# Other cuts for the last row of a streamed Poisson loss: x 3136, 768, 192 and t 1600, 1536, 576, 384 columns

## Chip, cores, metric

The kernel runs on one core of one Trainium2 chip. The metric is the device time of one execution, in microseconds (us). All executions that are compared here ran at a granted clock of 1.00; those of several rounds are classed as fast, and the four single runs at the end of the experiments have the state "unknown", which a single run of a one-core program always has. Kernels are compared only within the same rounds.

## The reference

```
batch, dim = 1024, 4096            # both inputs float32
loss = np.exp(log_input) - target * log_input
return np.mean(loss, axis=-1)      # 1024 numbers
```

Partition p holds rows 8p to 8p+7. Below, "row" means one of these eight, so a row is 128 partitions by 4096 columns, and x is `log_input`, t is `target`.

## The kernel before

SyncE issues all loads on one queue: rows 0 to 3 of x, then of t, rows 4 and 5, row 6, and the last row in seven pieces whose sizes TAIL sets (in units of d/32 = 128 columns). ScalarE takes the exponential of each x piece and sums it, VectorE multiplies each t piece with x and sums it. The sums of the last row's pieces stand behind t's last columns as six extra columns, against an x of -1.0 there, so that VectorE's closing instruction multiplies the last t piece and adds up all partial sums in one go.

```
TAIL = [("x", 24), ("t", 12), ("t", 12), ("x", 6), ("t", 5), ("x", 2), ("t", 3)]
# ... (cut)
    for what, w in TAIL:
        loads.append((what, at[what], w * d // 32))
        at[what] += w * d // 32
# ... (cut: buffers, semaphores, the loads, the loop over x)
    for j, (lo, w, i) in enumerate(t_work):
        row = lo // d
        x_load = next(ix for a, wx, ix in x_work if a + wx >= lo + w)
        if j == 0 or x_load > t_work[j - 1][2]:
            nc.vector.wait_ge(landed[x_load], 16)
        if j < n_t - 1:
            nc.vector.tensor_tensor_reduce(...).wait_op(landed[i], 16, "sem-ge")...
        else:
            nc.vector.wait_ge(ones_done, 1)
            nc.vector.wait_ge(exp_done, n_x - 1)
            nc.vector.wait_ge(prod_done, n_t - 2)
            nc.vector.tensor_tensor_reduce(
                out=place("t", lo, w + n_parts), ...
                accum_out=all_loss[:, last_row : last_row + 1],
            ).wait_op(last_ready, 18, "sem-ge").then_inc(loss_done, 1)
```

`last_ready` reaches 18 when the last load (16), the last exponential (1) and the last product before the closing one (1) are done. A product waits for its own t piece and for the x piece that covers its last column.

## Time and profile before

| | before |
|---|---|
| time, median of 6 runs | 84.05 us (84.01 to 84.12) |
| span of the profiled execution | 82.9 us |
| share of 16 DMA engines in use | 95.5% |
| VectorE, ScalarE busy | 43%, 40% |

From the page of the kernel before, the DMA queue (packets, MB, share of 16 engines' span) and the chain that ended last (shares of the span by engine, then by line):

```profile
q1 hardware_dynamic: 2016, 33.56, 95.5%
...
DMA 72%; DVE 18%; issue 4%; SPq 3%; ACT 1%
DMA t_big<-in_target_dram 49%; DMA x_big<-in_log_input_dram 23%; DVE t_big L175 17%; SPq L129 3%; DVE t_big L193 1%; ACT e_dump L155 1%; DVE parts L175 0%; SPq L127 0%; DVE all_loss L193 0%
```

The chain is transfers, with compute (18% VectorE) only where a load has to wait for a buffer to come free while other transfers still run. ACT's 1% at its end is the one piece of compute that stands between the last transfer of the chain (the load of x3) and the closing instruction.

### The profile page before, as it was taken

The page shows a single profiled execution, that of the slowest core. Times are in us where ns is not written, and L with a number is a line of the kernel's source. Part 1 is how long each engine was busy: PE and PEld are TensorE (multiplying, and loading weights), DVE is VectorE, ACT ScalarE, POOL GpSimd, SP SyncE. Part 2 cuts the span into 40 slices and gives each one's busy share as a digit, 9 for nine tenths or more (in the row PEclk, how much of TensorE's full clock was granted, in tenths as well). Part 3 has the DMA queues.
Part 4 walks back from the last instruction along what each step waited for, and adds up shares of the span by engine and source line. Part 5 has one row for each costly group of instructions (what it writes and reads, how often), then busy time and mean ns, then how long its engine had stood idle before and what let it go on. Part 6 is the DMA issues. An engine that isn't in the chain of part 4 may idle for free.

```text
span 82.9 us, 131 instructions
## 1 busy us (share of the span) xinstructions
DVE 35.6 (43%) x22; ACT 33.2 (40%) x35; POOL 0.3 (0%) x5
## 2 busy tenths in 40 slices
DVE  0000000000000000000099999999469996994992
ACT  0500000000399920000000897979793496019460
POOL 0000000000000000000000000000000000000000
DMA  9199999929999992999699799899899999999950
GB/s 506 63 443 506 506 506 506 443 127 443 506 506 506 506 443 127 443 506 506 269 490 474 316 474 490 380 411 490 364 403 435 443 435 393 433 397 421 393 184 2
DMA packets 2016, 33.56 MB, mean 405 GB/s; under 512 B 352, under 2 KB 608, under 8 KB 1120
## 3 DMA queue, kind: packets, MB, share of 16 engines
q1 hardware_dynamic: 2016, 33.56, 95.5%
HBM read 33.55 MB, written 0.00 MB: 405 GB/s over the span
## 4 chain that ended last, share of the span: by engine, by line
DMA 72%; DVE 18%; issue 4%; SPq 3%; ACT 1%
DMA t_big<-in_target_dram 49%; DMA x_big<-in_log_input_dram 23%; DVE t_big L175 17%; SPq L129 3%; DVE t_big L193 1%; ACT e_dump L155 1%; DVE parts L175 0%; SPq L127 0%; DVE all_loss L193 0%
## 5 line engine op out<-in xcount | busy, mean ns | idle before, releaser
L175 DVE CUSTOM_DVE_ANT_0 t_big<-t_big,x_big 128x4096 f32<-128x4096 f32 (+2 forms) x8 | 26.2, 3306 | 43.8 <-DMA t_big<-in_target_dram 43.6
L155 ACT ACTIVATE e_dump<-x_big 128x4096 f32<-128x4096 f32 (+3 forms) x8 | 21.8, 2730 | 24.2 <-DMA x_big<-in_log_input_dram 24.0
L175 DVE CUSTOM_DVE_ANT_0 t_mid<-t_mid,x_mid 128x4096 f32<-128x4096 f32 x2 | 8.8, 4424 | 2.0 <-DMA t_mid<-in_target_dram 2.0
L141 ACT ACTIVATE join_dump<-parts 128x2 f32<-128x2 f32 x7 | 1.4, 203 | 20.4 <-DVE parts L175 20.4
L155 ACT ACTIVATE e_dump<-x_mid 128x4096 f32<-128x4096 f32 x2 | 7.1, 3568 | 0.0
L155 ACT ACT_TABLE_LOAD x1 | 1.3, 1283 | 3.0 <-PEq L48 3.0
L155 ACT ACTIVATION_READ_ACCUMULATOR e_dump<-x_big 128x1 f32 x8 | 1.5, 186 | 0.0
L141 ACT ACTIVATION_READ_ACCUMULATOR join_dump<-parts 128x1 f32 x7 | 1.3, 186 | 0.0
L193 DVE CUSTOM_DVE_ANT_0 t_big<-t_big,x_big 128x390 f32<-128x390 f32 x1 | 0.6, 566 | 0.1
L175 DVE DVE_READ_ACCUMULATOR2_ANT parts<- 128x1 f32 x7 | 0.6, 81 | 0.0
L155 ACT ACTIVATION_READ_ACCUMULATOR e_dump<-x_mid 128x1 f32 x2 | 0.4, 186 | 0.0
L175 DVE DVE_READ_ACCUMULATOR2_ANT t_big<- 128x1 f32 x3 | 0.2, 83 | 0.0
L136 POOL MEMSET x_big<- 128x6 f32 x1 | 0.1, 103 | 2.5 <-POOLq L48 2.5
L227 POOL MEMSET const-bfloat16-1.0<- 128x1 bf16 x1 | 0.1, 101 | 0.0
L227 POOL MEMSET const-uint8-127<- 128x1 uint8 x1 | 0.1, 101 | 0.0
L227 POOL MEMSET const-float32-0.0<- 128x1 f32 x1 | 0.1, 98 | 0.2 <-issue 0.2
L227 POOL MEMSET const-float32-1.0<- 128x1 f32 x1 | 0.1, 98 | 0.0
L193 DVE DVE_READ_ACCUMULATOR2_ANT all_loss<- 128x1 f32 x1 | 0.1, 84 | 0.0
## 6 DMA issues: line engine op xcount, KB each, us to landing
x_mid<-in_log_input_dram SPq DMA_DIRECT2D x1, 4096.0 KB, 50.2
t_mid<-in_target_dram SPq DMA_DIRECT2D x1, 4096.0 KB, 59.5
x_big<-in_log_input_dram SPq DMA_DIRECT2D x1, 2048.0 KB, 19.8
t_big<-in_target_dram SPq DMA_DIRECT2D x1, 2048.0 KB, 24.3
x_big<-in_log_input_dram SPq DMA_DIRECT2D x1, 1536.0 KB, 15.3
t_big<-in_target_dram SPq DMA_DIRECT2D x2, 768.0 KB, 17.6
x_big<-in_log_input_dram SPq DMA_DIRECT2D x1, 384.0 KB, 18.8
t_big<-in_target_dram SPq DMA_DIRECT2D x1, 320.0 KB, 19.1
```

Of the source, the lines that this page charges most:

```text
L129: dma = nc.sync.dma_start(out=place(what, lo, w), in_=src[:, lo : lo + w])
L136: nc.gpsimd.memset(big["x"][:, 4 * d : 4 * d + n_parts], -1.0).then_inc(ones_done, 1)
L141: nc.scalar.activation(out=join_dump[:, 2 * row : 2 * row + 2], in_=parts[:, 2 * row : 2 * row + 2], func=ACT_F.Copy, scale=inv_d, accum_o ...
L155: nc.scalar.activation(out=e_dump[:, col : col + w], in_=place("x", lo, w), func=ACT_F.Exp, bias=0.0, scale=1.0, accum_out=parts[:, 2 * ro ...
L175: nc.vector.tensor_tensor_reduce(out=place("t", lo, w), in0=place("t", lo, w), in1=place("x", lo, w), scale=-1.0, scalar=0.0, op0=ALU.mult ...
L193: nc.vector.tensor_tensor_reduce(out=place("t", lo, w + n_parts), in0=place("t", lo, w + n_parts), in1=place("x", lo, w + n_parts), scale= ...
L227: nc = _bacc.Bacc("TRN2", target_bir_lowering=False, num_devices=1)
```

## The change

The intent is to let VectorE and ScalarE have less left to do once the last load has landed: the early pieces are made larger and the last x and t pieces before the closing one smaller, in finer units.

```
-TAIL = [("x", 24), ("t", 12), ("t", 12), ("x", 6), ("t", 5), ("x", 2), ("t", 3)]
+TAIL = [("x", 98), ("t", 50), ("t", 48), ("x", 24), ("t", 18), ("x", 6), ("t", 12)]
...
-        loads.append((what, at[what], w * d // 32))
-        at[what] += w * d // 32
+        loads.append((what, at[what], w * d // 128))
+        at[what] += w * d // 128
```

(An assertion on d changes with it.) In columns, in the order of the queue, x1 t1 t2 x2 t3 x3 t4 go from 3072, 1536, 1536, 768, 640, 256, 384 to 3136, 1600, 1536, 768, 576, 192, 384.

## The prediction

> **What bounds the kernel now.** I read the page's slices first, to see which resource is full.
>
> ```profile
> DVE  0000000000000000000099999999469996994992
> ACT  0500000000399920000000897979793496019460
> ...
> DMA  9199999929999992999699799899899999999950
> ...
> DMA packets 2016, 33.56 MB, mean 405 GB/s; under 512 B 352, under 2 KB 608, under 8 KB 1120
> ```
>
> The DMA engines are full from the first slice to the 38th; VectorE and ScalarE are busy 43% and 40% of the span and mostly wait. So the kernel is a 33.55 MB stream, and compute can only add what is left over once the last bytes have landed. That remainder is what the sizes of the last row's pieces set. Next I read the timeline of the last eight microseconds, which holds the whole argument (start, duration, engine and instruction, idle time before it):
>
> ```profile
> 74.36 2.73 ACT L155 ACTIVATE e_dump<-x_big 128x3072 f32<-128x3072 f32 x1 [4.38 <-DMA x_big<-in_log_input_dram]
> ...
> 76.24 1.76 DVE L175 CUSTOM_DVE_ANT_0 t_big<-t_big,x_big 128x1536 f32<-128x1536 f32 x1 [1.15 <-DMA t_big<-in_target_dram]
> ...
> 78.15 1.76 DVE L175 CUSTOM_DVE_ANT_0 t_big<-t_big,x_big 128x1536 f32<-128x1536 f32 x1
> 79.13 0.81 ACT L155 ACTIVATE e_dump<-x_big 128x768 f32<-128x768 f32 x1 [1.52 <-DMA x_big<-in_log_input_dram]
> ...
> 79.95 0.83 DVE L175 CUSTOM_DVE_ANT_0 t_big<-t_big,x_big 128x640 f32<-128x640 f32 x1
> 80.30 0.39 ACT L155 ACTIVATE e_dump<-x_big 128x256 f32<-128x256 f32 x1 [0.23 <-DMA x_big<-in_log_input_dram]
> 80.62 0.19 ACT L155 ACTIVATION_READ_ACCUMULATOR e_dump<-x_big 128x1 f32 x1
> 80.70 0.08 DVE L175 DVE_READ_ACCUMULATOR2_ANT t_big<- 128x1 f32 x1
> 80.84 0.57 DVE L193 CUSTOM_DVE_ANT_0 t_big<-t_big,x_big 128x390 f32<-128x390 f32 x1
> ```
>
> I call the pieces x1 t1 t2 x2 t3 x3 t4, in their order in the queue. The last semaphore increments of their loads stand in the trace at 74.34, 76.22, 78.13, 79.11, 79.93, 80.28 and 80.75 us. Each consumer starts some 0.02 us after its own landing (74.36, 76.24, 78.15, 79.13, 79.95, 80.30): the engines keep pace with the stream through all seven pieces. The closing instruction (the 390 columns of t4 and the partial sums) waits for three things, whose events in the trace are: t4 landed 80.745, product of t3 done 80.798, exponential of x3 done 80.818. It starts at 80.84. The chain of waits names the last of these:
>
> ```profile
> 61.30 18.97 DMA x_big<-in_log_input_dram
> 80.28 0.02 issue
> 80.30 0.52 ACT e_dump L155 x2
> 80.82 0.02 issue
> 80.84 0.57 DVE t_big L193
> ```
>
> The reader should see how little there is to win: with both other conditions met early, the closing instruction would start at 80.745 + 0.02 = 80.77, or 0.07 us sooner. That is 0.09% of 84.06 us.
>
> **What the Trainium skill says.**
> - "VectorE: DVE Perf Modes", section on the TRN2 errata for SBUF-source ops, gives (N+151)/0.96 ns for an fp32 tensor_tensor of N columns. The trace agrees, though our operation is a custom one: 1536 columns give 1757 ns (row: 1759), 640 give 824 (827).
> - "ScalarE: Activation LUTs", section "What ACT_TABLE_LOAD costs", gives 0.833 ns a column. The trace: (2735-815)/(3072-768) = 0.833.
> - "DMA: Bandwidth & Descriptors", section "How a descriptor splits into AXI transactions": a descriptor is cut into 256-byte transactions, and one that does not start on a 256-byte boundary fetches bytes it does not use. New widths and offsets are all multiples of 64 floats, or 256 bytes (3136x4 = 49x256, 1600x4 = 25x256, 576x4 = 9x256, 192x4 = 3x256), so this costs nothing by that account. The old ones are multiples of 512 bytes, so the trace of before cannot confirm it.
> - The same page, "Anatomy of one DMA", puts most of a transfer's fixed cost into confirming that the last byte landed. The trace shows such a lag: the last data packets of 1536 B end at 80.30 and the semaphore is complete at 80.75, so 0.45 us, and this lies behind the stream however it is cut.
>
> **The change part by part.** No instruction, byte, transfer or packet is added or removed: seven loads, three exponentials and four products before and after. Packets stay 128 for each load. Column totals stay 4096 for x and for t. What moves is where the cuts lie.
>
> *Landing times.* Load intervals in this stretch: 1536 columns took 1.88 and 1.91 us, 768 took 0.98, so (1.89-0.98)/768 = 1.19 ns a column plus some 0.07 us for each load. Measured in columns queued, the ends of the pieces move as follows: x1 3072 to 3136, t1 4608 to 4736, t2 6144 to 6272, x2 6912 to 7040, t3 7552 to 7616, x3 7808 to 7808, t4 8192 to 8192. So x1 lands 64x1.19 = 0.076 us later, t1, t2 and x2 each 0.152, t3 0.076; x3 and t4 land when they did. New landings: 74.42, 76.37, 78.28, 79.26, 80.00, 80.28, 80.75.
>
> *ScalarE.* x1 starts at 74.44 and is 64x0.833 = 53 ns longer; it and the join behind it are done near 77.7, long before x2. x2 starts at 79.28, unchanged in size. Before, its accumulator read ended at 80.06 (79.88+0.18), so now at 80.21. x3 lands at 80.28, so the idle time of 0.23 us in front of it shrinks to some 0.08 but does not vanish: x3 still starts at 80.30. Its 192 columns are 53 ns shorter. Its done event: 80.818-0.053 = 80.765. This part alone takes 0.053 us off the condition that comes last today.
>
> *VectorE.* t1 starts at 76.39 and is 64x1.042 = 67 ns longer, 1.826 us. Back to back, instructions of this kind start 4.35 us apart at a duration of 4.42 (45.79, 50.14 in the timeline), so the next can start 0.07 us before the recorded end: 76.39+1.826-0.07 = 78.15. t2 lands at 78.28, so it starts at 78.30: the stream still sets it, by 0.15 us. It frees the engine at 78.30+1.76-0.07 = 79.99. t3 lands at 80.00 and starts at 80.02 (80.025 without rounding), 0.075 later than before; its 576 columns are 67 ns shorter. Its done event: 80.798+0.076-0.067 = 80.807. This is the tight place: only 0.03 us separate the freed engine from the landing.
>
> *The closing instruction* has the same 390 columns (no piece was added, so there are still six partial sums) and the same 0.57 us. It now waits for the latest of 80.745 (t4), 80.765 (x3) and 80.807 (t3), instead of 80.818. Sum: 80.807-80.818 = -0.011 us. ScalarE's gain of 0.053 is cut to 0.011, because VectorE stands right behind it and moves 0.009 the wrong way. Everything after it, the closing instruction, the store and its landing, is unchanged. 84.06-0.01 = 84.05 us.
>
> **The rivals.**
> 1. *VectorE becomes the bound by more than this.* If t3 cannot start until the accumulator read of t2 has ended and its done event is out (before: 79.84+0.08 = 79.92, event at 79.93; shifted by 0.15, 80.08), it starts near 80.10 and its event comes near 80.88, so the closing instruction starts 0.06 us later than now. For it: t3 started just after that event in the trace of before. Against: t3's own landing was at 79.93 too, and the four products that ran with their data long landed (starts at 45.79, 50.14, 54.48, 65.22) each began together with the accumulator read before them. It would make 84.12.
> 2. *The new cuts slow the stream.* Widths become odd multiples of 256 bytes. If the memory or the engines prefer 512, packets of x1 and t1 would take longer than size predicts. Last-row traffic is 4.2 MB, about 11 us from 69.33 (first packet of x1) to 80.30; a slowdown of 1% in it costs 0.1 us, and a slowdown of 15%, or 1.7 us, would be needed for a 2% verdict. Against: packet times of before follow size with small remainders (12288 B took 462 ns, 6144 B 238, 3072 B 124, 2560 B 105), with no sign of a step at 2560, an odd multiple of 512. A mild form would give 84.15 to 84.3.
> 3. *The full gain.* If t3's done event came as early as x3's, the time would be set by t4's landing and 84.06-0.05 = 84.01 would come out; 83.99 is the floor while the stream is unchanged. Against: the 0.076 us by which t3 lands later is arithmetic on the queue's order.
> 4. *Hidden anyway.* A shift of a hundredth of a microsecond is below what separates chips or profiled executions (the profiled run took 84.23, the timed ones 84.04 to 84.06), so the measured difference may have either sign.
>
> **How the range and the chances follow.** The mechanism allows -0.07 to about +0.06 us, or 83.99 to 84.12. I widen this on both sides for the variation between executions and for a slight cost of the new cuts, to 83.94 to 84.16. A gain of over 2% (1.68 us) would need the stream to be shorter, and it moves the same bytes in the same number of packets: 0.005. A loss of over 2% needs a 15% slowdown of the last row's traffic: 0.01. The rest, 0.985, is within 2%.
>
> **What would show it right or wrong.** In the timeline of the changed kernel: t1 should start about 76.39, t2 78.30, x2 79.28, t3 80.02, x3 80.30 and the closing instruction 80.83, its releaser being VectorE's product instead of ScalarE's exponential. The exponentials should take 2.79, 0.81 and 0.33 us, the products 1.83, 1.76, 0.76 and 0.57. If t3 starts at 80.10, rival 1 holds. If x1's last packets (12544 B) take clearly more than 471 ns (462 plus 256 B at the 37 ns per KB between 12288 and 6144 B), or t4 lands later than 80.75, rival 2 holds. If x3 starts after 80.30, the shrunk idle time in front of it was too small. A time below 83.9 would mean that I have mistaken what bounds the end.

## The result, and the profile after

83.97 us (83.85 to 84.11, 6 runs) against 84.05 us (84.01 to 84.12, 6 runs). The ratio is 0.9989, with a 95% interval of 0.9976 to 1.0002. The interval includes 1. Ratios are the mean time of one kernel's runs over that of the other's of the same rounds, so not quite the ratio of the medians.

The timeline of the changed kernel, the part that answers to the one in the prediction (start, duration, engine and instruction, idle time before it):

```profile
74.10 2.79 ACT L155 ACTIVATE e_dump<-x_big 128x3136 f32<-128x3136 f32 x1 [4.44 <-DMA x_big<-in_log_input_dram]
...
76.05 1.83 DVE L175 CUSTOM_DVE_ANT_0 t_big<-t_big,x_big 128x1600 f32<-128x1600 f32 x1 [1.28 <-DMA t_big<-in_target_dram]
...
78.93 0.81 ACT L155 ACTIVATE e_dump<-x_big 128x768 f32<-128x768 f32 x1 [1.53 <-DMA x_big<-in_log_input_dram]
...
79.70 0.76 DVE L175 CUSTOM_DVE_ANT_0 t_big<-t_big,x_big 128x576 f32<-128x576 f32 x1
79.97 0.33 ACT L155 ACTIVATE e_dump<-x_big 128x192 f32<-128x192 f32 x1
...
80.50 0.57 DVE L193 CUSTOM_DVE_ANT_0 t_big<-t_big,x_big 128x390 f32<-128x390 f32 x1
```

The durations are those of the sum: 2.79, 1.83, 0.81, 0.76, 0.33 and 0.57 us. The formula that the prediction takes from the Trainium skill ("VectorE: DVE Perf Modes", on the errata) holds for the new widths too: (N+151)/0.96 gives 1824 ns for 1600 columns and 757 for 576, where the rows show 1.83 and 0.76 us. The chain of waits of the changed kernel at its end shows the predicted change of hands, from ScalarE's exponential to VectorE's product of t3 ("issue" is time in which the engine waited for nothing that the profile shows):

```profile
79.95 0.04 issue
80.00 0.05 DVEq L192
80.05 0.34 issue
80.38 0.09 DVE t_big L175
80.47 0.02 issue
80.50 0.57 DVE t_big L193
```

But all of the tail stands 0.3 us earlier than predicted, the closing instruction at 80.50 and not 80.83. Were that the work of the new cuts, the gain would be 0.3 us. It isn't: the shift is there from the first load on. The first exponential of both kernels, which waits for the first load only (rows 0 to 3, which the change doesn't touch), starts 0.30 us apart. Before:

```profile
22.10 3.59 ACT L155 ACTIVATE e_dump<-x_big 128x4096 f32<-128x4096 f32 x1 [17.84 <-DMA x_big<-in_log_input_dram]
```

After:

```profile
21.80 3.59 ACT L155 ACTIVATE e_dump<-x_big 128x4096 f32<-128x4096 f32 x1 [17.58 <-DMA x_big<-in_log_input_dram]
```

So a difference between two traces has to be read against a landmark inside each. I use two: the landing of the first load, and the landing of t4 (a landing is the last of a load's 16 semaphore increments in the trace). The time then falls into three parts: until the first load has landed; from there until t4 has landed (the stream); and the rest, which is the profiled execution's time less t4's landing. The last column is the start of the closing instruction less t4's landing, the overhang that the change is about. All 14 traces, in us:

| trace | time | first load landed | stream | rest | overhang |
|---|---|---|---|---|---|
| before, first | 84.23 | 22.08 | 58.67 | 3.48 | 0.096 |
| a_before | 83.90 | 21.73 | 58.68 | 3.49 | 0.096 |
| a2_before | 83.82 | 21.66 | 58.68 | 3.47 | 0.090 |
| a3_before | 83.98 | 21.76 | 58.73 | 3.49 | 0.105 |
| after, first | 83.89 | 21.77 | 58.67 | 3.45 | 0.058 |
| b_after | 84.02 | 21.88 | 58.66 | 3.48 | 0.100 |
| b2_after | 83.91 | 21.76 | 58.68 | 3.48 | 0.079 |
| b3_after | 83.96 | 21.83 | 58.69 | 3.45 | 0.053 |
| c_x_only | 83.97 | 21.74 | 58.65 | 3.57 | 0.186 |
| d_t_only | 84.89 | 21.78 | 58.72 | 4.39 | 1.003 |
| h_floor | 84.04 | 21.94 | 58.69 | 3.41 | 0.024 |
| e_double | 83.99 | 21.82 | 58.68 | 3.50 | 0.104 |
| f_odd | 84.09 | 21.82 | 58.79 | 3.48 | 0.090 |
| g_next | 83.94 | 21.81 | 58.63 | 3.50 | 0.144 |

The first load's landing ranges over 0.41 us, among the four traces of the unchanged kernel alone. The stream stays within 0.06 us of 58.67 in all but f_odd, and the rest hardly moves except where an experiment moves it. The means of the four traces each: rest 3.484 before, 3.464 after; overhang 0.097 before, 0.073 after. By these means the change is worth about 0.02 us, a quarter of the 0.08 us between the medians. This is an estimate and not more: the single traces overlap (an overhang of 0.090 to 0.105 before, 0.053 to 0.100 after), and four of each don't establish a difference of 0.02.

### The profile page after: what moved, and what is told of

The parts are those of the page before. It is cut to its first block, busy times and chain, and to the rows that moved or that the text cites. A ratio compares the mean times of both kernels' runs of the same rounds, so it can differ in the third digit from the quotient of the medians.

```text
span 82.5 us, 131 instructions
## 1 busy us (share of the span) xinstructions
DVE 35.6 (43%) x22; ACT 33.2 (40%) x35; POOL 0.3 (0%) x5
## 4 chain that ended last, share of the span: by engine, by line
DMA 72%; DVE 18%; issue 5%; SPq 3%; DVEq 0%
DMA t_big<-in_target_dram 49%; DMA x_big<-in_log_input_dram 23%; DVE t_big L175 17%; SPq L129 3%; DVE t_big L193 1%; DVE parts L175 0%; DVEq L192 0%; SPq L127 0%; DVE all_loss L193 0%
## 5 line engine op out<-in xcount | busy, mean ns | idle before, releaser
L175 DVE CUSTOM_DVE_ANT_0 t_big<-t_big,x_big 128x4096 f32<-128x4096 f32 (+3 forms) x8 | 26.2, 3308 | 43.5 <-DMA t_big<-in_target_dram 43.4
```

The source lines that it names most:

```text
L175: nc.vector.tensor_tensor_reduce(out=place("t", lo, w), in0=place("t", lo, w), in1=place("x", lo, w), scale=-1.0, scalar=0.0, op0=ALU.mult ...
```

## The experiments

**Control and repeat.** The kernel before against itself, and the changed kernel again, five rounds on one chip.

a_before, no edit:

> The kernel before, unchanged, as a control. Every theory expects a ratio of 1.000; how far it is off, and how far its single runs spread, is the noise against which the others are read. If the skew between DMA engines (in the first trace of before the 16th semaphore increment of each load came 0.27-0.33 us after the 15th, in the trace of after 0.08-0.10) is a matter of the execution and not of the cuts, this trace may show either value.

Measured: 83.97 us (83.90 to 84.07, 6 runs) against 84.09 of the same rounds, ratio 0.9986 (0.9963 to 1.0008). The kernel measured against itself shows the same "gain" as the change did. The last increment of a load came only 0.01 to 0.05 us after the 15th in this trace, against 0.27 to 0.31 in the first trace of the same kernel. So this lag does not come from the cuts.

b_after, no edit of the changed kernel:

> The changed kernel again. My theory (stream unchanged, only the three conditions of the closing instruction move): 0.01 to 0.03 us faster, ratio 0.9996 to 0.9999, hardly to be told from 1; in the trace the closing instruction starts 0.06 us after the landing of t4 (before: 0.095). Rival (the new cuts shorten the stream): ratio 0.999 or below again, the distance from the first data packet of x1 to the landing of t4 shorter by 0.05 us or more beyond the skew.

Measured: 84.01 us, ratio 0.9987 (0.9965 to 1.0009), beside the control's 0.9986. Times cannot tell the two kernels apart. The trace is a miss for the overhang: 0.100 us, not 0.06, with VectorE's product of t3 the last condition. The distance from t3's landing to t4's was 0.724 us here and 0.766 in the first trace of after; landings scatter by some hundredths, as much as the effect.

**Half of the change: x alone.**

```
-TAIL = [("x", 98), ("t", 50), ("t", 48), ("x", 24), ("t", 18), ("x", 6), ("t", 12)]
+TAIL = [("x", 98), ("t", 48), ("t", 48), ("x", 24), ("t", 20), ("x", 6), ("t", 12)]
```

> Only the cuts of x are moved (3136, 768, 192), t as before (1536, 1536, 640, 384). My theory: x3's exponential is 0.053 us shorter, but t3 lands 64 columns (0.076 us) later and is not shorter, so VectorE's t3 becomes the last condition: closing instruction 0.056 us later than before, ratio 1.0006. Rival (the exponential of x3 was the bound and only its length counts): 0.03 to 0.05 us faster, ratio 0.9995.

Measured: 84.15 us, ratio 1.0017 (0.9987 to 1.0046): the time decides nothing here. In the trace the overhang is 0.186, so 0.09 us more than before, with VectorE as the releaser: my theory's direction, more than its size, and against the rival. (From t3's landing to t4's it took 0.707 us here, where the sum gives 0.816 less 0.076, or 0.740.) The timeline of this kernel:

```profile
79.71 0.83 DVE L175 CUSTOM_DVE_ANT_0 t_big<-t_big,x_big 128x640 f32<-128x640 f32 x1
79.97 0.34 ACT L155 ACTIVATE e_dump<-x_big 128x192 f32<-128x192 f32 x1 [0.18 <-DMA x_big<-in_log_input_dram]
80.23 0.19 ACT L155 ACTIVATION_READ_ACCUMULATOR e_dump<-x_big 128x1 f32 x1
80.46 0.08 DVE L175 DVE_READ_ACCUMULATOR2_ANT t_big<- 128x1 f32 x1
80.58 0.57 DVE L193 CUSTOM_DVE_ANT_0 t_big<-t_big,x_big 128x390 f32<-128x390 f32 x1
```

ScalarE ends at 80.42 (80.23 and 0.19) and VectorE at 80.54. Shortening x3 is worth nothing as long as t3 is not shortened too.

**The other half: t alone.**

```
-TAIL = [("x", 98), ("t", 50), ("t", 48), ("x", 24), ("t", 18), ("x", 6), ("t", 12)]
+TAIL = [("x", 96), ("t", 50), ("t", 48), ("x", 24), ("t", 18), ("x", 8), ("t", 12)]
```

> Only the cuts of t are moved (1600, 1536, 576, 384), x as before (3072, 768, 256). t2 then ends at column 3136, beyond x1 (3072), so its product has to wait for x2. My theory: t2 starts near 79.2 (x2's landing, 64 columns later than before) in place of 78.15, VectorE has no slack to make it good, and the closing instruction comes some 0.8 us later: ratio 1.009 to 1.010. Rival (VectorE has slack, since it is busy 43% only): within 0.1 us of before.

Measured: 84.92 us, ratio 1.0104 (1.0078 to 1.0129), overhang 1.003, which is 0.91 us over that of before. This one is plain in the times. The timeline of this kernel:

```profile
78.91 0.81 ACT L155 ACTIVATE e_dump<-x_big 128x768 f32<-128x768 f32 x1 [1.58 <-DMA x_big<-in_log_input_dram]
79.02 1.76 DVE L175 CUSTOM_DVE_ANT_0 t_big<-t_big,x_big 128x1536 f32<-128x1536 f32 x1 [1.14 <-DMA x_big<-in_log_input_dram]
...
80.71 0.76 DVE L175 CUSTOM_DVE_ANT_0 t_big<-t_big,x_big 128x576 f32<-128x576 f32 x1
```

t2 now waits for x2 and no more for its own load, and t3 follows without a gap at 80.71. VectorE is busy 43% of the span, yet a delay of its last products comes out at the end: measured from t4's landing, t2 starts 1.11 us later than in the first trace of before, and 0.91 of that is left at the closing instruction. The 0.91 is over my 0.8 in part because t2 started 0.13 us after x2's landing (78.892 us) where I had taken 0.02. The rival is out. This is why x1 and t1, t2 had to be moved together: t1 and t2 end at column 3136, where x1 ends.

**The ceiling.** In the kernel before, the product of t3 and the exponential of x3 are cut to 32 columns; loads and waits stay. The result is wrong (relative error 0.020).

```
         row, col = lo // d, lo % d
+        if k == n_x - 1:
+            w = 32
...
+        if j == n_t - 2:
+            w = 32
         if j < n_t - 1:
```

> The kernel before with its cuts and loads, but the product of t3 and the exponential of x3 cover 32 columns only (a wrong result on purpose), so that both are done before t4 lands. It measures the most that any shifting of work between the pieces could gain. My theory: the closing instruction starts 0.02 to 0.03 us after the landing of t4 (before: 0.095), so 0.07 us are to be had, ratio 0.9992, and no more. Rival (something else than the three conditions holds the closing instruction back, such as its separate waits on its queue): it still starts over 0.06 us after the landing.

Measured: 84.02 us, ratio 1.0005 (0.9965 to 1.0045): the time decides nothing here. In the trace the overhang is 0.024 and the rest 3.41 us, as my theory had it. The timeline of this kernel:

```profile
80.32 0.19 ACT L157 ACTIVATION_READ_ACCUMULATOR e_dump<-x_big 128x1 f32 x1
80.65 0.56 DVE L197 CUSTOM_DVE_ANT_0 t_big<-t_big,x_big 128x390 f32<-128x390 f32 x1 [0.62 <-ACT e_dump L157]
```

The view names ScalarE as the releaser, but its done event came at 80.519, while the last increment on the semaphore that the closing instruction waits for is t4's landing, at 80.630. So the closing instruction waits for the data here and for no compute. The three conditions are all that holds it back. No choice of sizes can gain more than 0.097 less 0.024, or 0.07 us, with this closing piece.

**The change doubled.**

```
-TAIL = [("x", 98), ("t", 50), ("t", 48), ("x", 24), ("t", 18), ("x", 6), ("t", 12)]
+TAIL = [("x", 100), ("t", 52), ("t", 48), ("x", 24), ("t", 16), ("x", 4), ("t", 12)]
```

> The change doubled: x 3200, 768, 128; t 1664, 1536, 512, 384. My theory: t2 frees VectorE at about the time, or just after, t3 lands (0.15 us later than before), so t3 starts directly behind t2, its done event comes 0.11 to 0.12 us after the landing of t4 (before 0.053), and the closing instruction starts 0.13 to 0.15 us after that landing: 0.04 us slower than before, the releaser VectorE. Rival (smaller last pieces are always better): the closing instruction starts 0.03 us after the landing or sooner. In the times both lie within 0.1% of before, below the noise of 0.1%; the trace decides.

Measured: 84.05 us, ratio 1.0012 (0.9977 to 1.0046), overhang 0.104. A miss on the size: I expected 0.13 to 0.15. In the timeline t3 starts at 79.864, 0.023 us after its landing, and t2 had started 1.704 before; so t3 came just as VectorE was free and did not queue for 0.06 us behind t2 as I had worked out. The rival's 0.03 is missed further. In this one trace, going on in the same direction is no better than the change and about as good as before.

**Alignment.** Three of the five cuts are moved by one column: x1 to x2 at 3137, t1 to t2 at 1601, t3 to t4 at 3713.

```
-TAIL = [("x", 98), ("t", 50), ("t", 48), ("x", 24), ("t", 18), ("x", 6), ("t", 12)]
+TAIL = [("x", 3137), ("t", 1601), ("t", 1535), ("x", 767), ("t", 577), ("x", 192), ("t", 383)]
...
-        loads.append((what, at[what], w * d // 128))
-        at[what] += w * d // 128
+        loads.append((what, at[what], w * d // 4096))
+        at[what] += w * d // 4096
```

> The changed kernel with every cut but one moved by a single column (x 3137, 767, 192; t 1601, 1535, 577, 383), so that rows of t2, x2, t3, x3 and t4 start off every 256-byte and 512-byte boundary. If a start off a 256-byte boundary costs one more transaction,[...] their packets take up to 9 ns longer (256 B at 37 ns per KB) than size says, five loads by 8 packets by 9 ns make 0.36 us, ratio up to 1.004. If alignment costs nothing here: packet times of 470 (12548 B), 245 (6404 B), 237 (6140 B), 124 (3068 B), 96 (2308 B) ns as in the trace of after within 2 ns, and the time is that of after.

(A slip there: x3 and t3 still start on a 256-byte boundary, at columns 3904 and 3136, so only t2, x2 and t4 start off one, and the cost that was to be looked for is 3 by 8 by 9 ns, or 0.22 us.) Measured: 84.09 us, ratio 0.9997 (0.9969 to 1.0025). Median packet times: 471 ns (12548 B), 245 (6404 B), 234 (6140 B, off the boundary), 121 (3068 B, off), 94 (2308 B), 65 (1532 B, off), where the first trace of after has 470, 245, 238, 124, 95 and 68 for 12544, 6400, 6144, 3072, 2304 and 1536 B. No packet that starts off a boundary is slower. That the three kinds took 3 or 4 ns less is scatter: b2_after and b3_after show the same 234, 121 and 65 ns for packets that start on a boundary. But this is no test of the account that the Trainium skill gives ("DMA: Bandwidth & Descriptors", section "How a descriptor splits into AXI transactions"), and where the expectation called on that page it had it wrong: a start off a boundary fetches the bytes from the boundary below it, which here are 4 bytes. By that rule I estimate 24 transactions and 192 beats of 32 bytes for the 6140 B, the same as for 6144 B on a boundary, and the same holds for 3068 and 1532 B. A start far enough past a boundary to need a further transaction was not tried. This trace's stream of 58.79 us is the longest of all, but it had lost the time before x1: from x1's landing to t4's it took 6.343 us, against 6.352 to 6.370 in the four traces of after. So neither these shifts by a column nor the change's odd multiples of 256 bytes cost anything that shows.

**One step further.**

```
-TAIL = [("x", 98), ("t", 50), ("t", 48), ("x", 24), ("t", 18), ("x", 6), ("t", 12)]
+TAIL = [("x", 99), ("t", 51), ("t", 48), ("x", 23), ("t", 18), ("x", 6), ("t", 11)]
```

> A further step that my sums prefer: x 3168, 736, 192; t 1632, 1536, 576, 352. The closing instruction has 32 columns fewer (0.033 us shorter), t3 and x3 land 32 columns (0.038 us) later. My theory: the closing instruction starts about 0.02 us later relative to the landing of t4 than in the changed kernel, but is 0.033 us shorter: 0.01 to 0.02 us better than after, within noise in the times. Rival (t3 falls behind by more, as VectorE has no slack): it starts over 0.13 us after the landing.

Measured: 84.15 us, ratio 1.0004 (0.9976 to 1.0032), overhang 0.144, rest 3.50. A miss: the closing instruction is shorter (0.53 us in place of 0.57) but starts later by more than that, because t3 has as many columns as in the changed kernel and less time until t4 lands (0.679 us against 0.724 to 0.772). The rival's size was right, but not its reason: t3 started 0.02 us after its landing (79.784 after 79.761), so VectorE had slack enough to start it on time. The timeline of this kernel:

```profile
80.03 0.34 ACT L155 ACTIVATE e_dump<-x_big 128x192 f32<-128x192 f32 x1
80.30 0.19 ACT L155 ACTIVATION_READ_ACCUMULATOR e_dump<-x_big 128x1 f32 x1
80.47 0.08 DVE L175 DVE_READ_ACCUMULATOR2_ANT t_big<- 128x1 f32 x1
80.58 0.53 DVE L193 CUSTOM_DVE_ANT_0 t_big<-t_big,x_big 128x358 f32<-128x358 f32 x1
```

**More traces of the two kernels,** one look each, no edits.

> The kernel before again, for one more trace. In ten traces so far the landing of t4 lies 58.63 to 58.79 us after that of the first load, while the first load itself lands anywhere from 21.73 to 22.08; the time less t4's landing was 3.48 and 3.49 in the two traces of before. My theory (the 0.08 us between the medians is scatter of the first load): again 58.67 within 0.06 and 3.48 within 0.03, whatever the time. Rival (the cuts change the stream): in before the stretch of 58.67 is longer than in after by 0.05 or more.

> The changed kernel again, for one more trace. My theory: t4 lands 58.67 us after the first load within 0.06, and the time less t4's landing is 3.45 to 3.48, on average 0.01 to 0.03 below that of before; the closing instruction starts 0.06 to 0.10 us after t4's landing. Rival: a real gain of 0.08 would show as 3.40.

> The kernel before once more, with the same expectations as for the run before it of this kernel: 58.67 us within 0.06 from the landing of the first load to that of t4, and 3.48 us within 0.03 from there to the end.

> The changed kernel once more, with the same expectations as for the run before it of this kernel: 58.67 us within 0.06 from the landing of the first load to that of t4, and 3.45 to 3.48 us from there to the end.

Measured: 83.82 and 83.98 us for before, 83.91 and 83.96 for after. All four streams lie within the 0.06 us (58.68, 58.73, 58.68, 58.69). The rest is 3.47 and 3.49 before, 3.48 and 3.45 after (3.445 exactly, a hair below the range). None of the four traces of after has the 3.40 that a gain of 0.08 asks for. The stream alone averages 58.69 in the four traces of before and 58.67 in those of after; 0.02 us with single traces 0.06 apart is not enough to say that it differs.

## Why the prediction was right

- **The bound.** Right: the stream fills the span, and only the overhang is in play. h_floor shows both its cause and its ceiling. (The digits 1 and 2 in the DMA row that the prediction calls full are no gaps. The page counts a packet in the slice in which it starts; spread over the time that they took, the packets fill every slice from the second to the 38th.)
- **The number.** That 83.97 lies within the range says little about the mechanism: the unchanged kernel's own median was 83.97 in a_before. The sign "below 83.9" was too tight as well, since the unchanged kernel itself ran at 83.82, beside h_floor and in a2_before.
- **Landing times.** Right where it counts. In the four traces each, t3 to t4 took 0.829 us before and 0.752 after on average, 0.077 less; the sum had 0.076.
- **ScalarE's part.** x3's done event came 0.074 us after t4's landing before and 0.014 after, on average: 0.060 sooner, against 0.053 in the sum. The idle time ahead of x3 shrank but did not vanish in the timeline of after: x2's accumulator read began at 79.68 and x3 at 79.97.
- **VectorE's part.** t3's done event came 0.039 us after t4's landing before and 0.049 after: 0.010 later, against 0.009. As the sum said, VectorE takes the end over from ScalarE: x3's event is the later of the two in all four traces of before, t3's in all four of after. (One slip: the 0.03 us that the sum leaves there is the distance from the freed engine, 79.99, to t3's start. To t3's landing, 80.005, it is 0.015.)
- **The closing instruction.** The handover is shown; the size seems low, as far as four traces tell: by the same means, the last condition went from 0.074 (x3) to 0.049 (t3), so -0.025 us where the sum has -0.011. The term that was off is the lead of t3 over x3 before the change: I read 0.020 in one trace, and four traces have 0.035 on average.
- **Rival 1** (t3 waits until the accumulator read of t2 is out): false. In the first trace of after t3 starts at 79.697, and t2's done event comes at 79.717. In e_double, the tightest case, t3 starts at 79.864 and that event comes at 79.939.
- **Rival 2** (cuts that slow the stream): false, by the change's own packets, 470 ns for 12544 B where the sum allowed 471, and by the stream, 58.67 us on average against 58.69 before.
- **Rival 3** (the full gain): not reached; 0.024 of the 0.07 by the means.
- **Rival 4** (hidden in the scatter): right. The measured 0.08 us is no measure of the change, as the control's 0.9986 shows; the mechanism gives about a quarter of it. What makes the first load land earlier or later from one execution to the next stays open. The traces show one part of it: of the 0.30 us between the first traces of before and after, 0.19 is the lag of the first load's last increment behind its 15th (0.285 us against 0.098). No experiment here bore on why that lag differs.

## What to carry to other kernels

When the stream of loads sets the time, first measure the ceiling: cut the work that trails the last load to nothing and see when the closing instruction starts. Here it was 0.07 of 84 us, and three further choices of sizes could not be told from the kernel before by their times. Below the scatter of the times, compare traces from a landmark inside them (the landing of the last load), take several, and run the kernel against itself beside the change.

## What the Trainium skill lacked or had wrong

- "DMA: Bandwidth & Descriptors", section "Latency and other measured facts", says that DMA engines 7 and 15 are usually slower, but takes this for a matter of the software queue. I found no page that says how far a load's last engine can lag on the hardware queue, which is the one used here (q1 hardware_dynamic): the last increment came 0.27 to 0.31 us after the 15th in one execution and 0.01 to 0.05 in another of the same kernel. The records don't say which engine it was.
- I found no page on the scatter between executions of one kernel that streams its loads: the first load (8 MB) landed at 21.66 to 22.08 us, and the following stream took 58.63 to 58.79 us.
- I found no page with the time from a landing to the start of an instruction: 0.02 us where the instruction carries the wait itself (x1 in a_before landed at 74.009 and its exponential started at 74.03), 0.13 us where VectorE had a wait of its own queued ahead of the product (x2 in d_t_only landed at 78.892, t2 started at 79.02).
